# Paired 256-token blocks per PSUM bank, HGRN products on other engines, reordered small steps and placed tiles in a two-block model kernel

## The chip, the cores and the metric

One core of one Trainium2 chip. The metric is the device time of one execution in microseconds; a version is judged by the median of several executions. The profile is one further execution, taken by the hardware profiler. Its engines are TensorE (PE; its weight loads, PEld, overlap the matmuls), VectorE (DVE), ScalarE (ACT), GpSimd (POOL) and SyncE (SP, which issues the weight DMAs).

## The reference

`x` is [256 tokens, 1024]. All arithmetic is float32. The first block is a mixer and a swiglu; the second is HGRN2, swiglu, RG-LRU, swiglu; a norm stands ahead of each and at the ends of both blocks.

```python
h = rmsnorm(x, norm_mix)
proj = h @ w_in        # mamba2, block attention, forgetting attention, sliding window, gates
branches = [mamba2(...), moba(...), forgetting(...), sliding_window(...)]
x = x + sum_i(sigmoid(gate_i) * (branches[i] @ w_branch[i])) @ w_out
x = x + swiglu(rmsnorm(x), ...); x = rmsnorm(x, norm_final)
# HGRN2, 8 heads of 128:
q, fl, v, g = split(h @ hgrn_w_in); q = silu(q)
f = lb + (1 - lb) * sigmoid(fl); k = (1 - lb) * sigmoid(-fl)
S_t = diag(f_t) S_{t-1} + k_t v_t^T;  o_t = S_t^T q_t
x = x + (rmsnorm_per_head(o) * silu(g)) @ hgrn_w_out;  x = x + swiglu(rmsnorm(x), ...)
# RG-LRU:
y, u = split(h @ lru_w_in); uc = conv4(u)
r, i = sigmoid(blockdiag(uc, wa) + ba), sigmoid(blockdiag(uc, wx) + bx)
a = exp(-8 r softplus(-lam)); h_t = a h_{t-1} + sqrt(1 - a^2) i uc
x = x + (h_t * gelu(y)) @ lru_w_out; x = x + swiglu(rmsnorm(x), ...); out = rmsnorm(x, norm_final)
```

## The kernel before

The activations `x` stay on chip as two tiles of 128 tokens. Ahead of each stage `norm_input` (L199) transposes a quarter of x on TensorE, multiplies by the norm's weight on VectorE (`tsc`) and takes the sum of squares on ScalarE (L205). The norm's factor is not applied to h; it is applied where a product is evicted: as a column per token (`rstd`, L232, with the power on GpSimd, L246) or, where the tokens lie along the free axis, as a row over all partitions (`rrow`, made by L258 with two diagonal matrices `dg` and two small matmuls, L264).

Every large product is made at high precision of three matmuls per 128 rows of k: both operands are split into a rounded part and a rest (hh and hl for the activations, whi and wlo for the weights), and L154, L155, L156 are the three products (`mm3`). ScalarE casts whi and hh (L100), VectorE subtracts to wlo and hl (L101); `burst` sends the next four subtractions to GpSimd.

Weights come in units of 1 MB: a DMA on SyncE's queue into one of 4 raw buffers (`wunit`, L141), then two split tiles of 1024 columns each out of 4 (`weights`, L107). Products have two shapes. In `gemm_a` (L158) a 128 x 128 piece of h is stationary and 512 weight columns move; it serves the swiglus, the values, the gates and the output projections (where ah and al, oh and ol, loh and lol take the place of hh and hl). In `gemm_b` (L185) a 128 x 128 piece of weights is stationary and the 256 tokens of h move; each block of 128 output columns (`block_b`, L190) is 24 matmuls into the left half of a PSUM bank of its own, and is evicted by one VectorE product with `rrow`. There are 4 such banks (`acc`) and 4 more for transposes and small products (`tp`). `gemm_b` makes mamba's convolution inputs, the q and k of two attentions, HGRN's q and forget inputs (L779, L786), and RG-LRU's convolution and output gates (L930, L978).

The order of the work is set by a scheduler that runs when the kernel is built: it lists the instructions of each engine by priority (the order in which the code issues them), lets ready work of an idle engine go earlier, and is steered by `high_priority(offset)` (the splits of weights use 400, 150 in RG-LRU) and by `issue_after`, which forbids an instruction to stand ahead of another.

Around the change: `hgrn` (L748) evicts each block to one of three `u` buffers, takes a sigmoid on ScalarE (L781) and the product q on GpSimd (L782); for the forget block two sigmoids on ScalarE (L788, L789), then the affine steps on VectorE (L790, L791). `hgrn_scores` (L825) multiplies q and k on GpSimd (L834), rounds on ScalarE (L835), subtracts on GpSimd (L836), and runs levels of gated halves on VectorE (`G`, L876). `lru_rates` (L570) takes Exp and Ln of the decay parameters (L586); it is issued within the first swiglu, without a bound on how early it may go. `skew_bias` (L389) writes the bias table of 16 heads to DRAM (`relv`) and spreads it over 128 partitions into `skew` by two DMAs on GpSimd's queue, one for each attention that has such a bias (the first and the third); the attentions read their diagonals from it. `rows4` (L437) loads four heads' decay rows by a DMA on the same queue into one buffer. `conv` and `gate` in `lru` (L909) alternate four convolutions with the block-diagonal gates (L951) and the gate activations.

On-chip memory is given out pool by pool, in order: constants, x, hh and hl (`hp`), `small`, `tmp` (7168 bytes of a partition), `wraw` (32,768), `wspl`, and then the pools of a stage, such as `ffn` or `hgrn`. The weights' split tiles begin at a multiple of the tile size after `wraw`, so the distance from hh to them is the sum of the sizes between: hh and hl, `small`, `tmp` and `wraw`, 59,200 bytes.

```python
    def block_b(self, hk, wk, cs):
        n, m = len(hk), cs.stop - cs.start
        ps = self.acc()[:m, :S]
        with self.held():
            for k in range(n):
                self.mm3(ps, wk[k][0][:, cs], wk[k][1][:, cs], hk[k][0], hk[k][1], k == 0, k == n - 1)
        return ps
```

Of the kernel before, what the change touches and what calls it, by code (L numbers as in the profile page):

```python
# [20 lines left out]
EPS = 1e-6  # L21
NEG = -1.0e30
# [52 lines left out]
class Build:  # L75
    def __init__(self, tc, a):
# [8 lines left out]
        self.place = -1  # L85
        self.ahead = 400
# [111 lines left out]

    def norm_input(self, x, n, t, wcol, hi, lo, ss):  # L199
# [3 lines left out]
        junk = self.tmp.tile([P, 512], F32, tag="junk", name=self.nm("junk"), bufs=1)  # L203
        if ss is not None:
            nc.scalar.activation(junk, xc, AF.Square, accum_out=ss[:, t, n:n + 1])  # L205
# [26 lines left out]
    def rstd(self, ss, scale=1.0 / D):  # L232
# [3 lines left out]
        nc.vector.tensor_tensor(r, ss[:, :, 0], ss[:, :, 1], op=ALU.add)  # L236
        self.rsqrt(r, r, scale)
# [20 lines left out]
    def make_row(self, r):  # L258
        nc = self.nc
# [5 lines left out]
        rr = self.small.tile([P, S], F32, tag="rrow", name=self.nm("rrow"))  # L265
# [20 lines left out]
    def constants(self):  # L286
# [29 lines left out]
    def swiglu(self, hk, r, wg, g0, wu, u0, wd, x, finish, apart=0, aside=None):  # L316

        nc = self.nc
        with self.tc.tile_pool(name=self.nm("ffn"), bufs=1) as fp:
            ah = fp.tile([P, FF // P, S], F32R, name=self.nm("ah"))  # L320
            al = fp.tile([P, FF // P, S], F32R, name=self.nm("al"))
            for c0 in range(0, FF, 512):
                if c0 == 1024 and aside:
                    aside()
                n = min(512, FF - c0)
                psg, psu = self.gemm_pair(hk, wg, g0 + c0, wu, u0 + c0, n, early=c0 == 0)
                for t in range(2):
# [45 lines left out]
    def mixer(self, hk, r, rr, x, finish):  # L373
        nc, a, tc = self.nc, self.a, self.tc
        w_in = a["w_in"][0]
        with tc.tile_pool(name="yT", bufs=3) as ytp, tc.tile_pool(name="att", bufs=1) as at, \
# [12 lines left out]
            def skew_bias():  # L389
# [47 lines left out]
            def rows4(h0):  # L437
                rw = mp.tile([P, 4, S], F32, tag="rows", name=self.nm("rows"), bufs=1)
# [724 lines left out]
```

## Time and profile before

| | |
|---|---|
| Median of 3 runs | 1179.6 us (1176.96, 1179.6, 1179.66) |
| Profiled execution | 1177.61 us, span 1175.9 us |
| Mean granted clock of TensorE | 0.992 of full speed |
| TensorE busy | 1140.0 us (97% of the span), 6308 matmuls |
| VectorE busy | 737.0 us (63%) |
| ScalarE busy | 615.5 us (52%) |
| GpSimd busy | 82.1 us (7%) |
| HBM read | 200.64 MB, 174 GB/s over the span |

The span runs from the first to the last instruction of the profiled execution; its own time is 1.7 us longer. A busy TensorE is not TensorE at its peak: matmuls are pipelined, each record is longer than the distance to the next, so a pace is read from the starts. Idle time of an engine that nobody waits for costs nothing. The granted clock is the share of full speed that the chip gave TensorE in a stretch.

### The profile page before, as it was taken

To read this page: it belongs to the slowest core of one execution; us is meant where nothing else is said; L and a number is where in the kernel's file an instruction comes from. 1 tells how busy PE (TensorE), PEld (TensorE's weight loads), DVE (VectorE), ACT (ScalarE), POOL (GpSimd) and SP (SyncE) were. 2 spreads that over 40 slices of the span, in tenths; PEclk is the share of its full clock that TensorE was granted. 3 is DMA by queue.
4 is the path that set the end of the run, shared out by engine and by line. 5 is a ranking of instruction groups with operands and counts; after the bars stand their busy time and mean duration, and the time that the engine had idled before them with its cause. 6 is when DMAs were issued, how large, how long until landed. Compare 5 with 4: busy or idle time off the path is not lost.

```text
span 1175.9 us, 15771 instructions
## 1 busy us (share of the span) xinstructions
PE 1140.0 (97%) x6308; PEld 981.0 (83%) x6308; DVE 737.0 (63%) x971; ACT 615.5 (52%) x909; POOL 82.1 (7%) x87
## 2 busy tenths in 40 slices
PE   7999999999999999998999999999999879999997
PEld 7899897888888888888989878888889778888886
DVE  6976555566575555556898676555458767555552
ACT  6646647654455444446542465444446876444441
POOL 1100010000000000006520140000000000000000
PEclk9999999999999999999999999999999989999999
DMA  9785245446555555456353337554554536555440
GB/s 299 188 265 190 87 144 188 162 147 206 184 192 184 181 186 186 172 179 204 112 179 108 108 108 251 183 195 177 197 167 156 179 120 214 185 179 179 163 159 36
DMA packets 120761, 202.78 MB, mean 172 GB/s; under 512 B 4244, under 2 KB 44437, under 8 KB 120688
## 3 DMA queue, kind: packets, MB, share of 16 engines
q1 hardware_dynamic: 117264, 192.59, 50.0%
q0 software_dynamic: 2992, 8.56, 2.6%
q8 instruction: 49, 0.80, 0.3%
q10 hardware_dynamic: 432, 0.63, 0.2%
q14 instruction: 24, 0.20, 0.0%
HBM read 200.64 MB, written 4.25 MB: 174 GB/s over the span
## 4 chain that ended last, share of the span: by engine, by line
PE 84%; ACT 6%; DVE 5%; DMA 3%; issue 2%; POOLq 0%; POOL 0%; SPq 0%; ACTq 0%; DVEq 0%
PE acc L154 25%; PE acc L156 25%; PE acc L155 25%; DMA raw<-in_w_in_dram 2%; DVE wlo L101 2%; PE tp L274 2%; PE tp L865 2%; ACT whi L100 2%; PE tp L695 1%; PE tp L208 1%; DVE G L876 1%; PE tp L724 1%; PE tp L732 0%; DMA rows<-acd 0%; PE tp L731 0%
## 5 line engine op out<-in xcount | busy, mean ns | idle before, releaser
L101 DVE TENSOR_TENSOR wlo<-raw,whi 128x1024 fp32r<-128x1024 f32 (+3 forms) x364 | 444.2, 1225 | 303.5 <-ACT whi L100 296.9
L100 ACT CAST whi<-raw 128x1024 fp32r<-128x1024 f32 (+3 forms) x372 | 382.0, 1033 | 363.2 <-PE acc L156 294.3
L156 PE MATMUL acc<-whi,hl 128*128 128x512 f32 (+2 forms) x832 | 316.2, 381 | 0.0
L155 PE MATMUL acc<-wlo,hh 128*128 128x512 f32 (+2 forms) x832 | 313.7, 377 | 1.3 <-DVE wlo L101 1.3
L154 PE MATMUL acc<-whi,hh 128*128 128x512 f32 (+2 forms) x832 | 311.3, 378 | 1.3 <-ACT whi L100 1.1
L155 PEld LDWEIGHTS acc<-wlo,hh 128*128 128x128 f32 x832 | 156.4, 188 | 31.0 <-DVE wlo L101 2.4
L154 PEld LDWEIGHTS acc<-whi,hh 128*128 128x128 f32 x832 | 156.3, 188 | 28.7 <-ACT whi L100 1.9
L156 PEld LDWEIGHTS acc<-whi,hl 128*128 128x128 f32 x832 | 156.4, 188 | 28.1 <-issue 0.7
L154 PE MATMUL acc<-hh,whi 128*128 128x256 f32 (+1 forms) x496 | 142.2, 289 | 9.5 <-ACT rg L951 4.5
L156 PE MATMUL acc<-hh,wlo 128*128 128x256 f32 (+1 forms) x496 | 141.6, 287 | 1.9 <-DVE wlo L101 1.9
L155 PE MATMUL acc<-hl,whi 128*128 128x256 f32 (+1 forms) x496 | 141.8, 287 | 0.3 <-DVE hl L101 0.3
L154 PEld LDWEIGHTS acc<-hh,whi 128*128 128x128 f32 (+1 forms) x496 | 95.7, 194 | 12.7 <-ACT rg L951 4.7
L155 PE MATMUL acc<-wlo,ah 128*128 128x512 f32 x264 | 103.1, 391 | 0.0
L156 PE MATMUL acc<-whi,al 128*128 128x512 f32 x264 | 102.6, 389 | 0.0
L154 PE MATMUL acc<-whi,ah 128*128 128x512 f32 x264 | 102.5, 390 | 0.0
L156 PEld LDWEIGHTS acc<-hh,wlo 128*128 128x128 f32 (+1 forms) x496 | 95.6, 193 | 2.8 <-DVE wlo L101 2.6
L155 PEld LDWEIGHTS acc<-hl,whi 128*128 128x128 f32 (+1 forms) x496 | 95.8, 193 | 1.3 <-DVE hl L101 0.6
L156 PEld LDWEIGHTS acc<-whi,al 128*128 128x128 f32 x264 | 49.6, 188 | 10.2
L154 PEld LDWEIGHTS acc<-whi,ah 128*128 128x128 f32 x264 | 49.6, 188 | 10.1
L155 PEld LDWEIGHTS acc<-wlo,ah 128*128 128x128 f32 x264 | 49.6, 188 | 10.1
L100 ACT CAST ah<-tp 128x512 fp32r<-128x512 f32 (+1 forms) x36 | 19.8, 550 | 33.9 <-PE tp L274 33.9
L330 ACT ACTIVATE sg<-acc,rstd 128x512 f32<-128x512 f32 (+1 forms) x36 | 23.3, 648 | 20.4 <-PE acc L156 20.4
(306 smaller groups left out, 1250.8 us busy)
## 6 DMA issues: line engine op xcount, KB each, us to landing
raw<-in_ffn_w_in_dram SPq DMA_DIRECT2D x44, 1024.0 KB, 5.2
raw<-in_w_in_dram SPq DMA_DIRECT2D x33, 1024.0 KB, 5.1
raw<-in_ffn_w_out_dram SPq DMA_DIRECT2D x20, 1024.0 KB, 5.1
raw<-in_hgrn_w_in_dram SPq DMA_DIRECT2D x16, 1024.0 KB, 5.5
raw<-in_w_ffn_gate_dram SPq DMA_DIRECT2D x11, 1024.0 KB, 5.1
raw<-in_w_ffn_up_dram SPq DMA_DIRECT2D x11, 1024.0 KB, 5.2
raw<-in_w_ffn_down_dram SPq DMA_DIRECT2D x10, 1024.0 KB, 5.1
raw<-in_w_branch_dram SPq DMA_DIRECT2D x8, 1024.0 KB, 5.1
```

Of the source, the lines that this page charges most:

```text
L100: self.nc.scalar.copy(hi, src)
L101: (eng or self.nc.vector).tensor_tensor(lo, src, hi.bitcast(F32), op=ALU.subtract)
L154: mm(ps, sh, mh, start=start, stop=False)
L155: mm(ps, sh, ml, start=False, stop=False)
L156: mm(ps, sl, mh, start=False, stop=stop)
L208: last = nc.tensor.transpose(ps[:, j * P:(j + 1) * P], xc[:, j * P:(j + 1) * P], self.ident)
L274: nc.tensor.transpose(ps[:, j * P:(j + 1) * P], src[:, j * P:(j + 1) * P], self.ident)
L330: nc.scalar.activation(sg[:, :n], psg[t][:, :n], AF.Silu, scale=r[:, t:t + 1])
L695: nc.tensor.matmul(ps[par][:, jj * W:(jj + 1) * W], qT[pr, 2 * gi + jj, qt * P:(qt + 1) * P], kT(2 * gi + jj)[pr, :W], start=True, stop=True)
L724: nc.tensor.transpose(ps[:, i * P:(i + 1) * P], sp[:, i, b * P:(b + 1) * P], self.ident)
L865: nc.tensor.matmul(ps[:, c:c + 64], k[:, h, ts], q[:, h, ts].rearrange("p (n u l) -> p n u l", u=2, l=L)[:, :, 1], start=True, stop=True)
L876: nc.vector.tensor_tensor(G2, G[:, :, 0], G[:, :, 1], op=ALU.mult)
```

## The change

`gemm_b` makes its two blocks in one bank, block by block within each k, and all evictions of it are one VectorE product over both (`times_row`). `new_h` takes tiles 128 elements longer and puts h at element 96 (STILL, for the three swiglus) or 16 (MOVING, for the mixer, HGRN and RG-LRU). The opening's squares come behind its four transposes; the factor chains `rstd` and `row` run at priority offset 600. `lru_rates` and HGRN's lower bounds (`hgrn_floors`, now in the constant pool) stand behind the second chunk's silu of the first swiglu. The second skew copy is issued behind the first attention; the decay rows get two buffers. In HGRN the products q, pr and the subtraction pl go from GpSimd to VectorE, the affine steps from VectorE to ScalarE, the scaling of x by the earlier norm's factor from GpSimd to ScalarE and behind the projections; oh and ol come first in the pool, the masks ahead of the projections; u has two buffers of twice the size. RG-LRU's convolution inputs are two double tiles; a spacer of 32 elements (`apart`) follows.

```diff
+STILL, MOVING = 96, 16
...
     def gemm_b(self, hk, w, c0, nblk):
         wk = self.wunit(w, 0, 8, c0, nblk * P)
-        return [self.block_b(hk, wk, slice(b * P, (b + 1) * P)) for b in range(nblk)]
+        ps = self.acc()
+        n, mm = len(hk), self.nc.tensor.matmul
+        with self.held():
+            for k, (h, l) in enumerate(hk):
+                for b in range(nblk):
+                    o, (wh, wl) = ps[:, b * S:(b + 1) * S], (u[:, b * P:(b + 1) * P] for u in wk[k])
+                    mm(o, wh, h, start=k == 0 and b == 0, stop=False, skip_group_check=True)
+                    mm(o, wh, l, start=False, stop=False, skip_group_check=True)
+                    mm(o, wl, h, start=False, stop=k == n - 1, skip_group_check=True)
+        return ps[:, :nblk * S].rearrange("p (b s) -> p b s", s=S)
+
+    def times_row(self, out, ps, rr):
+        self.nc.vector.tensor_tensor(out, ps, rr.unsqueeze(1).to_broadcast([P, ps.shape[1], S]), op=ALU.mult)
...
-    def new_h(self):
-        hi = [self.hp.tile([P, 4, S], F32R, tag=f"hh{n}", name=self.nm("hh")) for n in range(2)]
-        lo = [self.hp.tile([P, 4, S], F32R, tag=f"hl{n}", name=self.nm("hl")) for n in range(2)]
+    def new_h(self, place):
+        def part(tag):
+            t = self.hp.tile([P, 4 * S + 128], F32R, tag=tag, name=self.nm(tag[:2]))
+            return t[:, place:place + 4 * S].rearrange("p (k s) -> p k s", s=S)
+        hi, lo = ([part(f"{u}{n}") for n in range(2)] for u in ("hh", "hl"))
...
-        nc.vector.tensor_tensor(r, ss[:, :, 0], ss[:, :, 1], op=ALU.add)
-        self.rsqrt(r, r, scale)
+        with self.tc.high_priority(offset=self.rush):
+            nc.vector.tensor_tensor(r, ss[:, :, 0], ss[:, :, 1], op=ALU.add)
+            self.rsqrt(r, r, scale)
...
-        rr = self.small.tile([P, S], F32, tag="rrow", name=self.nm("rrow"))
+        rr = self.small.tile([P, S], F32, tag="rrow", name=self.nm("rrow"), bufs=1)
...
                 if c0 == 1024 and aside:
-                    aside()
+                    with self.tc.issue_after(last.ins):
+                        aside()
...
-                for g in range(2):
-                    nc.gpsimd.dma_start(skew[g], relv[:, g].unsqueeze(1).to_broadcast([8, P, NV]))
+                copies(0)
...
-                rw = mp.tile([P, 4, S], F32, tag="rows", name=self.nm("rows"), bufs=1)
+                rw = at.tile([P, 4, 384], F32, tag="sp", name=self.nm("rows"), bufs=2)[:, :, :S]
...
+            copies(1)
             qT2, kT2, v2 = load_qkv(3080)
...
+            def made(g):
+                q, k, f = (hp.tile([P, 4, S], F32, tag=n, name=self.nm(n), bufs=2) for n in ("hq", "hk", "hf"))
+                for c in range(2):
+                    h0 = 4 * g + 2 * c
+                    hs = slice(2 * c, 2 * c + 2)
+                    u = hp.tile([P, 2, S], F32, tag="u", name=self.nm("u"), bufs=2)
+                    self.times_row(u, self.gemm_b(hk, w, h0 * P, 2), rr())
+                    sg = hp.tile([P, 2, S], F32, tag="sgq", name=self.nm("sgq"), bufs=1)
+                    nc.scalar.activation(sg, u, AF.Sigmoid)
+                    nc.vector.tensor_tensor(q[:, hs], u, sg, op=ALU.mult)
+                    u = hp.tile([P, 2, S], F32, tag="u", name=self.nm("u"), bufs=2)
+                    self.times_row(u, self.gemm_b(hk, w, D + h0 * P, 2), rr())
+                    nc.scalar.activation(f[:, hs], u, AF.Sigmoid)
+                    nc.scalar.activation(k[:, hs], u, AF.Sigmoid, scale=-1.0)
+                    for i in range(2):
+                        h, fj, kj = h0 + i, f[:, 2 * c + i], k[:, 2 * c + i]
+                        nc.scalar.activation(fj, fj, AF.Identity, scale=om[:, h:h + 1], bias=lb[:, h:h + 1])
+                        nc.scalar.activation(kj, kj, AF.Copy, scale=om[:, h:h + 1])
+                return q, k, f
+            qkf = [made(g) for g in range(2)]
+            for t in range(2):
+                nc.scalar.activation(x[:, t], x[:, t], AF.Copy, scale=rf[:, t:t + 1])
...
-        nc.gpsimd.tensor_tensor(pr, q.rearrange("p h t -> p (h t)"), k.rearrange("p h t -> p (h t)"), op=ALU.mult)
-        nc.scalar.copy(ph, pr)
-        nc.gpsimd.tensor_tensor(pl, pr, ph.bitcast(F32), op=ALU.subtract)
+        nc.vector.tensor_tensor(pr, q.rearrange("p h t -> p (h t)"), k.rearrange("p h t -> p (h t)"), op=ALU.mult)
+        self.split(ph, pl, pr)
...
-            xins = self.conv_inputs(lp, 4)
+            xins = self.conv_inputs(lp, 2)
+            lp.tile([P, 32], F32, name="apart")
...
-            begin(col["norm_mix"])
+            begin(col["norm_mix"], MOVING)
             for n in range(2):
                 for t in range(2):
-                    finish(n, t)
+                    self.norm_input(x, n, t, state["w"], state["hi"], state["lo"], None)
+            for n in range(2):
+                for t in range(2):
+                    self.square(x[:, t, n * 512:(n + 1) * 512], state["ss"][:, t, n:n + 1])
```

## Rows read from the trace of the kernel before

**Rows 1.** The page: busy us, share of the span, instructions.
```profile
PE 1140.0 (97%) x6308; PEld 981.0 (83%) x6308; DVE 737.0 (63%) x971; ACT 615.5 (52%) x909; POOL 82.1 (7%) x87
```

**Rows 2.** TensorE's waits: what waited, releaser, us in total, times, longest us.
```profile
PE acc L154 <- ACT rg L951: 5.3, 2, 4.5
...
PE acc L154 <- ACT uh L100: 4.0, 1, 4.0
...
PE acc L154 <- DVE u L779: 2.7, 1, 2.7
```

**Rows 3.** Stretches: us, busy PE, PEld, DVE, ACT, POOL, granted clock, DMA share, GB/s.
```profile
8.40:10.40 2.00, 0.01 (x1) 0.01 (x1) 1.62 (x7) 2.00 (x7) 0.00 (x0) 1.00 1.09 354
70.80:72.10 1.30, 0.04 (x2) 0.03 (x1) 0.69 (x3) 1.29 (x4) 0.00 (x0) 1.00 1.03 395
...
554.60:558.00 3.40, 3.40 (x19) 3.40 (x20) 2.42 (x7) 2.06 (x6) 3.40 (x4) 0.62 0.73 217
570.00:613.00 43.00, 40.16 (x263) 35.46 (x261) 41.77 (x57) 20.86 (x31) 15.06 (x8) 1.00 0.46 148
909.40:970.00 60.60, 49.38 (x339) 46.34 (x338) 42.53 (x60) 49.09 (x75) 0.00 (x0) 0.92 0.45 145
```

**Rows 4.** Timeline of TensorE (start, us): 512-column matmuls, 34 of hh, 25 of ah.
```profile
1059.86 0.39 PE L154 MATMUL acc<-whi,hh 128*128 128x512 f32 x1
...
1067.41 0.39 PE L154 MATMUL acc<-whi,hh 128*128 128x512 f32 x1
...
1132.93 0.39 PE L154 MATMUL acc<-whi,ah 128*128 128x512 f32 x1
...
1138.37 0.39 PE L154 MATMUL acc<-whi,ah 128*128 128x512 f32 x1
```

**Rows 5.** Timeline of TensorE: 25 matmuls of gemm_b in HGRN, 25 in RG-LRU.
```profile
561.76 0.28 PE L154 MATMUL acc<-hh,whi 128*128 128x256 f32 x1
...
564.48 0.28 PE L154 MATMUL acc<-hh,whi 128*128 128x256 f32 x1
...
900.88 0.28 PE L154 MATMUL acc<-hh,whi 128*128 128x256 f32 x1
...
903.70 0.28 PE L154 MATMUL acc<-hh,whi 128*128 128x256 f32 x1
```

**Rows 6.** Timeline of ScalarE in the opening.
```profile
6.74 1.28 ACT L586 ACT_TABLE_LOAD   x1
...
9.89 0.44 ACT L100 CAST whi<-raw 128x320 fp32r<-128x320 f32 x1
```

**Rows 7.** DMA issues (KB each, median us to landing): 36 to 80 us, then the page.
```profile
raw<-in_w_in_dram SPq DMA_DIRECT2D x6, 1024.0 KB, 16.3
...
raw<-in_w_in_dram SPq DMA_DIRECT2D x33, 1024.0 KB, 5.1
```

**Rows 8.** Groups, 537 to 613 us: busy us, mean ns, idle before and its releaser.
```profile
L100 ACT CAST whi<-raw 128x1024 fp32r<-128x1024 f32 x22 | 22.9, 1047 | 11.1 <-PE acc L155 5.7 <-issue 4.3 <-PE acc L156 1.1
...
L876 DVE TENSOR_TENSOR G<-hf 128x512 f32<-128x512 f32 x2 | 4.9, 2456 | 0.0
L836 POOL TENSOR_TENSOR pl<-pr,ph 128x1024 fp32r<-128x1024 f32 x2 | 4.8, 2416 | 1.9 <-ACT ph L835 1.9
...
L790 DVE TENSOR_SCALAR hf<-hf,om,lb 128x256 f32<-128x256 f32 x8 | 3.9, 482 | 2.0 <-ACT hf L788 2.0
...
L791 DVE TENSOR_SCALAR hk<-hk,om 128x256 f32<-128x256 f32 x8 | 3.2, 403 | 0.0
L789 ACT ACTIVATE hk<-u 128x256 f32<-128x256 f32 x8 | 3.2, 402 | 0.0
...
L845 DVE TENSOR_TENSOR hq<-hq,hf 128x1024 f32<-128x1024 f32 x2 | 2.4, 1210 | 0.0
```

**Rows 9.** Timeline of VectorE: the norm's factor in RG-LRU and its first use.
```profile
889.18 0.15 DVE L236 TENSOR_TENSOR rstd<-ss 128x2 f32<-128x2 f32 x1
...
897.32 1.08 DVE L930 TENSOR_TENSOR xin<-acc,rrow 128x256 f32<-128x256 f32 x3
```

More of the change, by code (lines that the diff above doesn't have):

```diff
@@ L85, in __init__ @@
         self.place = -1
+        self.rush = 600
         self.ahead = 400
@@ L196, in block_b, with square @@
         return ps
+    def square(self, xc, out):
+        junk = self.tmp.tile([P, 512], F32, tag="junk", name=self.nm("junk"), bufs=1)
+        self.nc.scalar.activation(junk, xc, AF.Square, accum_out=out)
     def norm_input(self, x, n, t, wcol, hi, lo, ss):
@@ L258, in make_row, with row_of @@
     def make_row(self, r):
+        with self.tc.high_priority(offset=self.rush):
+            return self.row_of(r)
+    def row_of(self, r):
         nc = self.nc
@@ L512, in mixer @@
             kd = at.tile([P, S], F32, name="kd")
-            for ps in self.gemm_b(hk, w_in, 5136, 1):
-                nc.vector.tensor_tensor(kd, ps, rr(), op=ALU.mult)
+            self.times_row(kd.unsqueeze(1), self.gemm_b(hk, w_in, 5136, 1), rr())
             dv = at.tile([P, 2, P], F32, name="dv")
@@ L568, in mixer, with hgrn_floors @@
             gp.__exit__(None, None, None)
+    def hgrn_floors(self):
+        nc = self.nc
+        self.floors = lb, om = [self.const.tile([P, 8], F32, name=n) for n in ("lb", "om")]
+        lbp = self.col["hgrn_lb_2"]
+        lt = self.small.tile([P, 2, 8], F32, tag="lt", name="lt", bufs=1)
+        nc.vector.tensor_tensor(lb, lbp[:, 0:8], lbp[:, 8:16], op=ALU.max)
+        for i in range(2):
+            nc.vector.tensor_tensor(lt[:, i], lbp[:, i * 8:(i + 1) * 8], lb, op=ALU.subtract)
+        nc.scalar.activation(lt, lt, AF.Exp)
+        nc.vector.tensor_tensor(om, lt[:, 0], lt[:, 1], op=ALU.add)
+        nc.vector.reciprocal(om, om)
+        nc.vector.tensor_tensor(lb, lt[:, 0], om, op=ALU.mult)
+        nc.vector.tensor_tensor(om, lt[:, 1], om, op=ALU.mult)
     def lru_rates(self):
@@ L592, in conv_inputs @@
     def conv_inputs(self, pool, n):
-        xins = [pool.tile([P, S + 3], F32, name=self.nm("xin")) for _ in range(n)]
+        xins = [pool.tile([P, 2, S + 3], F32, name=self.nm("xin")) for _ in range(n)]
         for xin in xins:
-            self.nc.vector.memset(xin[:, 0:3], 0.0)
+            self.nc.vector.memset(xin[:, :, 0:3], 0.0)
         return xins
@@ L610, in mamba @@
         bcT = mp.tile([P, 4, S], F32, name="bcT")
-        xins = self.conv_inputs(mp, 2)
+        xins = self.conv_inputs(mp, 1)
+        cmask = mp.tile([P, 3, P], F32, name="cmask")
+        nc.gpsimd.memset(cmask, 1.0)
+        for j in (0, 2):
+            nc.gpsimd.affine_select(cmask[:, j], cmask[:, j], pattern=[[1, P]], compare_op=ALU.is_ge,
+                                    fill=0.0, base=0, channel_multiplier=-1)
         for b in (4, 6, 0, 2):
-            for j, ps in enumerate(self.gemm_b(hk, w_in, 512 + b * P, 2)):
+            xin2 = xins[0]
+            self.times_row(xin2[:, :, 3:], self.gemm_b(hk, w_in, 512 + b * P, 2), rr())
+            for j in range(2):
                 blk = b + j
-                xin = xins[j]
-                nc.vector.tensor_tensor(xin[:, 3:], ps, rr(), op=ALU.mult)
+                xin = xin2[:, j]
                 cv = mp.tile([P, S], F32, tag="cv", name=self.nm("cv"), bufs=2)
@@ L976, in out @@
             def out(n):
-                for i, ps in enumerate(self.gemm_b(hk, w, n * 256, 2)):
-                    nc.vector.tensor_tensor(yg[:, 2 * n + i], ps, rr(), op=ALU.mult)
+                self.times_row(yg[:, 2 * n:2 * n + 2], self.gemm_b(hk, w, n * 256, 2), rr())
             def gelu(n):
```

107 lines of the change are left out of this document (35 added, 72 removed).

## The prediction

> **What bounds the kernel now.** I read the busy shares first, then TensorE's waits, its stretches, and last the pace inside one stretch. TensorE is busy 97% of the span [rows 1], so a part of this change can pay in three ways only: a wait of TensorE goes, a clock drop that follows a wait goes, or the matmuls themselves come closer together. VectorE, ScalarE and GpSimd matter where they hold TensorE up.
>
> The waits are few and have places [rows 2]: 5.3 us and 4.0 us behind ScalarE in the RG-LRU mixer, 2.7 us behind a VectorE eviction (u) in HGRN. The stretches show what each costs [rows 3]. In the opening TensorE does nothing for 2.0 us while ScalarE is busy for all of them. At 70.8 us it does nothing for 1.3 us. In the 3.4 us after the wait for u, from 554.6, the granted clock is 0.62 (between the two levels, 1.2 and 2.4 GHz) and 19 matmuls pass, so a wait is paid twice. From 570 to 613 VectorE is busy 41.77 of 43 us and TensorE lacks 2.84: there VectorE sets the pace. From 909.4 to 970 TensorE is busy 49.38 of 60.6 us.
>
> The pace shows a fourth loss that no wait names. Starts of 512-column matmuls with h as the stationary operand lie (1067.41 − 1059.86)/33 = 228.8 ns apart; in the down projection, fed by ah and al, (1138.37 − 1132.93)/24 = 226.7 ns [rows 4]. Same shape, same weights' buffers, no waits. What differs is where the stationary tile lies: by the pool sizes hh starts 59,200 bytes before the weight tiles, 64 over a multiple of 256; ah an exact multiple.
>
> **The change, part by part.** The sum is made against the profiled execution's 1177.61 us (span 1175.9); the median of the runs is 1179.6, so 2 us of the answer is scatter that I do not correct for.
>
> *Places (−3.8).* With STILL, hh of the three swiglus comes 59,904 bytes before the weights, an exact multiple of 256; with MOVING the distance stays at 64 over one, so the mixers gain nothing. The swiglus' in-projections have 3 × 2 × 5 full chunks × 8 k × 2 token tiles × 3 = 1440 such matmuls: 1440 × 2.1 ns = 3.0 us. Their 256-column rests are 3 × 2 × 8 × 2 × 3 = 288 matmuls. For these narrow ones the trace has no row that differs by place alone; two HGRN and RG-LRU stretches run at 2.72/24 = 113.3 and 2.82/24 = 117.5 ns [rows 5], so between 0 and 288 × 4.2 ns = 1.2 us; I take half, 0.6. Moving oh first in its pool puts it at an exact multiple too: 96 matmuls at 2.1 ns, 0.2. The ends: nothing, and 4.4.
> The trace says that distance matters [rows 4]. The Trainium skill, "SBUF — State Buffer", section "SBUF: two separate sides", says that PE waits for nobody on the memory's engine side; by that rule places are worth nothing and the sum is 3.8 us smaller. No run here varies the place alone yet.
>
> *Opening (−1.5).* ScalarE's squares and the Ln table load for the RG-LRU rates (1.28 us) stand ahead of the first weight cast, at 9.89 us [rows 6]. The change puts the squares behind and ties the rates and the HGRN floors to the first swiglu. The idle 2.0 us [rows 3] bound the gain; below, the factor r now comes later, but it is first needed when a bank is to be evicted, and with priority 600 it precedes the bulk of the casts. Late next is the weight DMA, which runs at the full 1.09 share there; so 1.5, ends 0 and 2.0. In the swiglu the moved table load costs ScalarE 1.3 us, which is hidden beside matmuls.
>
> *Bias copies (−1.0).* In 36 to 80 us the two skew copies (8 × 128 × 383 values, 1.5 MB each) and the weights share the DMA engines: a 1 MB weight takes 16.3 us, 5.1 over the kernel [rows 7]. TensorE's 1.3 us [rows 3] follow. One copy is moved behind the first attention, where it passes that attention's bias and row loads on the GpSimd queue; the third attention, a whole attention later, needs it. The scheduler may still put it right behind the first, since GpSimd is idle. Ends 0 and −2.5 (wait and clock), I take −1.0. The rows' second buffer lets a 0.5 MB load start earlier, on the same crowded engines: 0.
>
> *HGRN (−6.0).* Two blocks per bank: a block is 24 matmuls, 2.72 us [rows 5], so four banks hold 21.7 us of TensorE's work in place of 10.9, and the wait for u at 551.8 goes: 2.7. Its clock drop goes too: 19 matmuls took 3.4 us, at 113.3 ns they take 2.15: 1.25. VectorE in 537 to 613 loses the affine steps, 8 × 0.48 + 8 × 0.40 = 7.1 us, and gains pr and pl, 4 × 1.21 = 4.8, and q, 4 × 0.61 (half the 1024-wide row) = 2.4 [rows 8]. So far even. But GpSimd's pl takes 2.42 beside it, and VectorE's 512-wide G takes 2.46 where a 1024-wide product takes 1.21 [rows 8]: with GpSimd out of the way each of two such G gives back about 1.8 us, 3.7 together, and sixteen evictions become eight. Of the 2.84 that TensorE lacks I take 2.0 (ends 0 and 2.84). ScalarE takes 16 × 0.40 = 6.4 us and two 1024-wide scalings of x at a cast's 1.05 [rows 8], 8.5 in all; in 570 to 613 it is busy 20.86 of 43 [rows 3], so they are hidden, but see the last rival. The pair's eviction waits for the second block, 2.72 us later: hidden as long as a bank is free. Ends of the whole: −7 and, by that rival, a loss.
>
> *RG-LRU (−2.5).* The factor's sum is at 889.18, the first eviction that needs it at 897.32 [rows 9], 8 us in which finished blocks keep their banks. Priority pulls this chain forward, and wide evictions save VectorE starts. But the waits of 5.3 and 4.0 us are behind ScalarE, which loses nothing here: its gate activations, scans and casts stay. Ends: +2.7 (a pair's wait that lands once on the convolution) and −9.3 (both waits); I take about a quarter.
>
> *Nothing.* Floors in the constant pool, the causal mask in the mamba pool, HGRN's masks ahead of its projections on GpSimd's queue (which the change empties), one row buffer, wide evictions in mamba and attention: TensorE has work queued beside each, and loses more only where the row buffer is rewritten before its last reader, which ends a stage earlier. The interleaved order of gemm_b changes which tile is read after which; two paces occur already [rows 5], and 57 blocks × 24 matmuls × 4.2 ns is 5.7 us between all fast and all slow, so ±5.7 at the most, taken as 0.
>
> Sum: −3.8 − 1.5 − 1.0 − 6.0 − 2.5 = −14.8, which gives 1162.8, so **1163 us**.
>
> **Rivals.**
> *Given back.* Where ScalarE or VectorE sets the pace, earlier work only waits later: opening, bias, VectorE's relief and RG-LRU give nothing; places and the bank remain, 3.8 + 2.7 + 1.25. For: ScalarE busy 2.00 of 2.00 and VectorE 41.77 of 43 in their stretches [rows 3]. Against: the removed work stands exactly there. 1170 us. Chance 0.16.
> *Places worth nothing.* The 2.1 ns come from something else that ah and hh do not share. Against: same shape, 33 and 24 matmuls at an even pace [rows 4]. 1177.6 − 11.0 = 1167 us. Chance 0.05. (This is also what the page named above would say.)
> *More than that.* Opening and bias in full, and RG-LRU's stalls nearly all, since its clock drop goes with them: 0.5 + 1.5 + 6.8 more, 1154 us. For: each wait there drags a low clock. Chance 0.09.
> *Slower.* In HGRN ScalarE works in order. The affine steps and sigmoids can stand behind weight casts that wait for TensorE to free a weight tile, TensorE's next unit waits for a bank, the bank for u, and u has two buffers now. Then each of the eight units waits a block, 2.72 us [rows 5], and HGRN's gain is gone: 1177.6 − 8.8 + 8 × 2.72 = 1190.6. It turns the sign from 6 units on (1185); with seven, **1188 us**. For: HGRN's casts already stand 5.7 us behind matmuls [rows 8]; against: ScalarE is half idle [rows 3] and two wide buffers hold as much as four narrow ones. Chance 0.10, a third of it under six units.
>
> **How the numbers follow.** The forecast has 0.60, its own range 1154 to 1171 from the ends above. A measurement of this kernel tells 0.3% (3.5 us) from no change, so faster ends at 1176.1 and slower begins at 1183.1. Forecast, places and more are faster (0.74); of "given back" 0.11 is faster and 0.05 within; of "slower" 0.07 is slower and 0.03 within: 0.85, 0.08, 0.07. The range leaves out the slower rival (0.10), half of "more" and the tails: 1150 to 1177.
>
> **What would show it.** Right: L154 starts 226.7 ns apart in the three in-projections; no wait for u; GpSimd with no wide products in HGRN, its 512-wide G near 0.7 us; a first weight cast before 9 us; the weights' landing below 16 us in 36 to 80. Wrong: TensorE waits in HGRN that end with ScalarE's sigmoid or affine step; a pace of gemm_b at 117 ns throughout; RG-LRU's two waits unchanged or longer.

## The result and the profile after

The changed kernel took 1158.33 us (median of 4 runs, 1156.59 to 1160.06), the kernel before in the same comparison 1178.88: a ratio of 0.9828, 95% interval 0.9808 to 0.9848. That is 20.5 us faster; the forecast was 1163 in 1150 to 1177. The direction and the range held, the sum was 4.7 us short, and not where a reader of the prediction would look for it.

The profiled execution took 1156.59 us, the fastest of the four, with a span of 1154.5. Six stages end with a residual addition on VectorE. Its last one in each stage, in the timeline of VectorE (start in us, duration):

```profile
343.71 0.69 DVE L380 TENSOR_TENSOR x<-acc,x 128x512 f32<-128x512 f32 x1 [0.28 <-PE acc L158]
...
531.00 0.69 DVE L380 TENSOR_TENSOR x<-acc,x 128x512 f32<-128x512 f32 x1 [0.67 <-PE acc L158]
...
681.46 0.68 DVE L380 TENSOR_TENSOR x<-acc,x 128x512 f32<-128x512 f32 x1
...
868.66 0.68 DVE L380 TENSOR_TENSOR x<-acc,x 128x512 f32<-128x512 f32 x1
...
961.84 0.69 DVE L380 TENSOR_TENSOR x<-acc,x 128x512 f32<-128x512 f32 x1
...
1147.79 0.69 DVE L380 TENSOR_TENSOR x<-acc,x 128x512 f32<-128x512 f32 x1 [1.23 <-PE acc L158]
```

In the kernel before:

```profile
350.17 0.69 DVE L355 TENSOR_TENSOR x<-acc,x 128x512 f32<-128x512 f32 x1 [0.29 <-PE acc L156]
...
538.09 0.69 DVE L355 TENSOR_TENSOR x<-acc,x 128x512 f32<-128x512 f32 x1 [0.67 <-PE acc L156]
...
698.91 0.68 DVE L355 TENSOR_TENSOR x<-acc,x 128x512 f32<-128x512 f32 x1
...
886.80 0.68 DVE L355 TENSOR_TENSOR x<-acc,x 128x512 f32<-128x512 f32 x1
...
982.27 0.69 DVE L355 TENSOR_TENSOR x<-acc,x 128x512 f32<-128x512 f32 x1
...
1169.17 0.69 DVE L355 TENSOR_TENSOR x<-acc,x 128x512 f32<-128x512 f32 x1 [1.23 <-PE acc L156]
```

The differences of neighbours give each stage its share, beside what the prediction had for it:

| Stage | before | after | change | forecast |
|---|---|---|---|---|
| mixer with the opening | 350.2 | 343.7 | −6.5 | −2.5 |
| three swiglus | 187.9, 187.9, 186.9 | 187.3, 187.2, 186.0 | −2.3 | −3.6 |
| HGRN | 160.8 | 150.5 | −10.4 | −6.2 |
| RG-LRU | 95.5 | 93.2 | −2.3 | −2.5 |

Each column is one execution, and the one after the change is the fastest of its four. In e1 to e3, e11 and e12 below, whose edits leave HGRN alone, that stage took 151.4 us. RG-LRU took 93.6 to 95.0 in e1 to e3, e6, e7 and e11, whose edits leave it alone, and 97.8 in e10, which is the kernel before with an edit in the mixer. So about 1 us of HGRN's gain hangs on the pace of this one execution (told of at the end), and RG-LRU's gain lies anywhere between 0.5 and 4.6.

The page's first part shows TensorE busy for 10 us less and GpSimd for 30% less [rows 1]:

```profile
PE 1129.9 (98%) x6308; PEld 975.1 (84%) x6308; DVE 725.5 (63%) x932; ACT 622.9 (54%) x915; POOL 57.1 (5%) x73
```

Of TensorE's waits [rows 2] the one for u is gone; the two behind ScalarE stay, one longer, one shorter:

```profile
PE acc L156 <- ACT rg L990: 5.9, 2, 5.1
...
PE acc L156 <- ACT uh L102: 2.5, 2, 2.2
```

The stretches that answer to [rows 3] (us, busy PE, PEld, DVE, ACT, POOL, granted clock, DMA share, GB/s):

```profile
8.20:10.40 2.20, 1.84 (x9) 1.06 (x8) 2.20 (x7) 2.20 (x6) 0.19 (x1) 1.00 1.09 364
70.00:80.00 10.00, 10.00 (x85) 9.78 (x84) 8.25 (x14) 4.37 (x6) 0.00 (x0) 1.00 0.98 315
...
560.00:597.00 37.00, 37.00 (x244) 33.48 (x242) 36.73 (x51) 25.68 (x36) 0.00 (x0) 1.00 0.59 191
880.00:949.00 69.00, 60.55 (x438) 57.12 (x438) 54.29 (x77) 57.09 (x86) 0.00 (x0) 0.95 0.46 146
```

In HGRN's projections and values TensorE is now busy all the time, although VectorE is as full as it was. The RG-LRU stretch still lacks 8.45 us.

HGRN's groups of instructions answer to [rows 8] (busy us, mean ns, idle before):

```profile
L835 ACT ACTIVATE hf<-hf,lb,om 128x256 f32<-128x256 f32 x8 | 4.3, 589 | 0.0
L836 ACT ACTIVATE hk<-hk,om 128x256 f32<-128x256 f32 x8 | 3.6, 496 | 0.0
...
L914 DVE TENSOR_TENSOR G<-hf 128x512 f32<-128x512 f32 x2 | 1.4, 710 | 1.1 <-ACT hf L835 1.1
```

G went from 2456 to 710 ns, as forecast. The affine steps cost 589 and 496 ns on ScalarE; the prediction had taken 402.

The pace, in the last swiglu's in-projection: 34 wide and 49 narrow matmuls, first and last of each (timeline of TensorE).

```profile
1020.58 0.39 PE L156 MATMUL acc<-whi,hh 128*128 128x512 f32 x1
...
1028.06 0.39 PE L156 MATMUL acc<-whi,hh 128*128 128x512 f32 x1
...
1080.05 0.28 PE L156 MATMUL acc<-whi,hh 128*128 128x256 f32 x1
...
1085.81 0.28 PE L156 MATMUL acc<-whi,hh 128*128 128x256 f32 x1
```

Wide: 7.48/33 = 226.7 ns, against 228.8 [rows 4]. Narrow: 5.76/48 = 120.0 ns.

ScalarE's queue in the opening, against [rows 6]:

```profile
7.71 0.63 ACT L218 ACTIVATE junk<-x 128x512 f32<-128x512 f32 x1
...
8.34 0.44 ACT L102 CAST whi<-raw 128x320 fp32r<-128x320 f32 x1
```

The first weight cast comes 1.55 us earlier. But the fourth square (`junk`) still stands ahead of it: the scheduler put the squares back where they were. It did the same with the copies (timeline of GpSimd's queue):

```profile
44.92 2.22 POOL L429 DMA_DIRECT2D skew<-relv  x2 [4.38 <-DMA relv<-rv]
```

Both skew copies go out together. Two of the change's moves were thus not made at all, and the mixer gained more than twice its forecast.

The norm's factor in RG-LRU (timeline of VectorE, against [rows 9]):

```profile
871.02 0.16 DVE L262 TENSOR_TENSOR rstd<-ss 128x2 f32<-128x2 f32 x1
...
880.50 0.69 DVE L204 TENSOR_TENSOR xin<-acc,rrow 128x512 f32<-128x512 f32 x1 [0.71 <-PE acc L199]
```

9.5 us from the sum to the first eviction, where it was 8.1: the eviction now waits for its second block. With the priority offset at 0 (e4) the same two lie as far apart, 877.18 to 886.65 us, so the priority of the factor brought nothing here.

### The profile page after: what moved, and what is told of

It is laid out like the page before. It is cut to its first block, busy times and chain, and to the rows that moved or that the text cites. A ratio compares the mean times of both kernels' runs of the same rounds, so it can differ in the third digit from the quotient of the medians.

```text
span 1154.5 us, 15679 instructions
## 1 busy us (share of the span) xinstructions
PE 1129.9 (98%) x6308; PEld 975.1 (84%) x6308; DVE 725.5 (63%) x932; ACT 622.9 (54%) x915; POOL 57.1 (5%) x73
## 3 DMA queue, kind: packets, MB, share of 16 engines
q1 hardware_dynamic: 117264, 192.59, 50.9%
## 4 chain that ended last, share of the span: by engine, by line
PE 92%; ACT 4%; DVE 2%; issue 1%; DMA 0%; SPq 0%; POOLq 0%; POOL 0%; ACTq 0%
PE acc L158 24%; PE acc L156 24%; PE acc L157 24%; PE acc L198 4%; PE acc L197 4%; PE acc L199 4%; PE tp L304 2%; PE tp L903 2%; ACT whi L102 1%; PE tp L743 1%; PE tp L228 1%; DVE wlo L103 1%; PE tp L772 1%; PE tp L780 0%; PE tp L779 0%
## 5 line engine op out<-in xcount | busy, mean ns | idle before, releaser
L103 DVE TENSOR_TENSOR wlo<-raw,whi 128x1024 fp32r<-128x1024 f32 (+3 forms) x364 | 438.1, 1210 | 299.3 <-ACT whi L102 292.6
L199 PE MATMUL acc<-hh,wlo 128*128 128x256 f32 x456 | 128.0, 281 | 0.0
L198 PE MATMUL acc<-hl,whi 128*128 128x256 f32 x456 | 127.8, 281 | 0.0
L197 PE MATMUL acc<-hh,whi 128*128 128x256 f32 x456 | 127.4, 281 | 0.0
L199 PEld LDWEIGHTS acc<-hh,wlo 128*128 128x128 f32 x456 | 86.3, 189 | 0.4 <-issue 0.3
L198 PEld LDWEIGHTS acc<-hl,whi 128*128 128x128 f32 x456 | 86.3, 189 | 0.4
L197 PEld LDWEIGHTS acc<-hh,whi 128*128 128x128 f32 x456 | 86.1, 190 | 0.6 <-issue 0.3
```

Source lines behind the costliest of these rows:

```text
L103: (eng or self.nc.vector).tensor_tensor(lo, src, hi.bitcast(F32), op=ALU.subtract)
L197: mm(o, wh, h, start=k == 0 and b == 0, stop=False, skip_group_check=True)
L198: mm(o, wh, l, start=False, stop=False, skip_group_check=True)
L199: mm(o, wl, h, start=False, stop=k == n - 1, skip_group_check=True)
```

## The experiments

All medians below are of 4 or more runs, each compared with runs of the kernel before on the same chip; the changed kernel stands at 1158.33. The kernel before had medians of 1176.9 to 1178.9 us in these groups, so a microsecond between two groups means nothing.

### Places: e1, e8 and e9

```diff
-STILL, MOVING = 96, 16
+STILL, MOVING = 16, 16
```

> The changed kernel with STILL set to 16, so that h of the swiglus lies 64 bytes over a multiple of 256 from the weights, as before the change. Theory (place decides the pace): starts of the 512-column matmuls with stationary h go from 226.7 back to 228.8 ns, 1440 x 2.1 = 3.0 us lost; the 288 narrow ones, which the changed kernel runs at 120.0 where before they ran at 117.8, give 0.6 back; in all +2.4 us on 1158.3. Rival (place is worth nothing, the swiglus gain by something else): the paces stay at 226.7 and 120.0 and the time within 0.5 us.

1160.57 us (ratio 0.9853, 0.9839 to 0.9868): 2.2 us slower. The same matmuls in its timeline:

```profile
1024.43 0.39 PE L156 MATMUL acc<-whi,hh 128*128 128x512 f32 x1
...
1031.98 0.39 PE L156 MATMUL acc<-whi,hh 128*128 128x512 f32 x1
...
1084.20 0.28 PE L156 MATMUL acc<-whi,hh 128*128 128x256 f32 x1
...
1089.85 0.28 PE L156 MATMUL acc<-whi,hh 128*128 128x256 f32 x1
```

7.55/33 = 228.8 ns and 5.65/48 = 117.7 ns. Place decides the pace, and it does so with opposite signs for these two widths. The rival that places are worth nothing falls.

The mixers' places, `MOVING`, were then set to an exact multiple (e8) and to a distance of 192 (e9).

```diff
-STILL, MOVING = 96, 16
+STILL, MOVING = 96, 96
```

> The changed kernel with MOVING set to 96 as well, so that h of the mixer, HGRN and RG-LRU lies an exact multiple of 256 bytes from the weights. Theory (place decides the pace of both shapes, and an exact multiple is good for 512 columns and bad for 256, as the swiglus' rests at 120.0 show): the 768 wide matmuls of these stages go from 228.8 to 226.7 ns, 1.6 us won; the 57 x 24 = 1368 narrow ones from 113 to 118 up to 120, 3 to 9 us lost; the time rises by 2 to 7 us. Rival (for narrow matmuls with the weights stationary an exact multiple is as good as for wide ones): 1 to 2 us faster.

1162.82 us (0.9873, 0.9858 to 0.9888), 4.5 slower. Narrow matmuls in HGRN run 120.0 ns apart, wide ones there mostly at 227 (median). The theory holds.

```diff
-STILL, MOVING = 96, 16
+STILL, MOVING = 96, 48
```

> The changed kernel with MOVING set to 48: the distance from h to the weights in the mixer, HGRN and RG-LRU is 192 over a multiple of 256 where it was 64, so seen from the weights 64 where it was 192. So far narrow matmuls ran at 120.0 for 0, at 117.8 for 64 with h stationary, and at 113 or 118 for the changed kernel's place with the weights stationary; wide ones at 226.7 for 0 and 228.8 for 64. Theory (each distance has one pace per shape, whichever operand is stationary): the narrow ones go to 118 throughout, about +3 us. Rival (what counts is the order of the two): another pace, up to 3 us faster if all run at 113.

1162.60 us (0.9875, 0.9854 to 0.9896), 4.3 slower: narrow ones at 118 (median) in HGRN, RG-LRU and the mixer, as the theory said, and the wide ones of the mixer and HGRN at 233 to 234, which it had not asked. Its profile also holds 1.6 us of the clock drop that is told of at the end. So 16 is the best of the three for the moving side, and 96 for the still side, of those tried.

### The opening: e2 and e4

```diff
                 if c0 == 1024 and aside:
-                    with self.tc.issue_after(last.ins):
-                        aside()
+                    aside()
```

> The changed kernel without the bound that ties the RG-LRU rates and the HGRN floors to the first swiglu, so that they may go early again. Theory (the opening's gain is the table load that left ScalarE's queue; the squares are still ahead of the first weight cast in the trace after): the first weight cast goes back from 8.3 us by about 1.5, TensorE's first product with it, and the time rises by 2.5 to 3.5 us. Rival (the gain is the factor's priority and the squares' new place): under 0.5 us.

1164.67 us (0.9887, 0.9872 to 0.9902): 6.3 us slower, twice the theory. ScalarE's timeline shows where both halves come from:

```profile
6.46 1.28 ACT L626 ACT_TABLE_LOAD   x1
...
9.61 0.44 ACT L102 CAST whi<-raw 128x320 fp32r<-128x320 f32 x1
...
74.02 1.05 ACT L102 CAST whi<-raw 128x1024 fp32r<-128x1024 f32 x1 [4.11 <-DMA raw<-in_w_in_dram]
74.97 0.52 ACT L698 ACTIVATE mt<-mt 128x384 f32<-128x384 f32 x1
```

The table load pushes the first cast to 9.61, which is 1.27 us. The rest is lost at 70 to 80 us: the skew copies go out at 50.9 in place of 44.9 us, the weights that share the DMA engines with them come later, ScalarE's cast waits 4.11 us for them at 74.02, and mamba's mask exponential (`mt`), which needs no weights, is queued behind it. TensorE waits 1.8 us for that mask, and its clock falls: over the stretch from 70 to 80 us it is 0.93, with TensorE busy 8.19 us, against 1.00 and 10.00 above.

```diff
-        self.rush = 600
+        self.rush = 0
```

> The changed kernel with priority offset 0 in place of 600 for the norm factors. Theory (the factor chains are hidden; RG-LRU's gain of 2.8 us comes from paired evictions): within 1 us of 1158.3. Rival (the earlier factor is what RG-LRU, HGRN and the opening gained by): +2 to +4 us, in the first 30 us of the stages that start with a row factor.

1163.41 us (0.9877, 0.9861 to 0.9894), 5.1 slower. "Within 1 us" was wrong, and so is the rival's place: RG-LRU's stage is no slower than in the other experiments. Its first product starts at 8.72 us, no later than the changed kernel's. Beside the changed kernel's profile it has lost 3 us by 180 us, by the same course as e2 (copies at 50.4 us, a wait for the mask of 1.1 us), and 1.6 at 180 to 190 in a clock drop that is told of at the end; the rest lies within the scatter of the stages.

### The stall at 70 us: e3, e10 and e11

```diff
-                rw = at.tile([P, 4, 384], F32, tag="sp", name=self.nm("rows"), bufs=2)[:, :, :S]
+                rw = mp.tile([P, 4, S], F32, tag="rows", name=self.nm("rows"), bufs=1)
```

> The changed kernel with one buffer for the decay rows, as before. Theory (TensorE's wait at 70.8 us before the change stood behind the second load of the rows, which waited for the one buffer, not behind crowded weight loads): the second load goes back to some 60 to 67 us, TensorE waits 1 to 2 us for a small VectorE product of those rows and its clock falls after; +3.5 to +4.5 us. Rival (the gain at 70 to 80 us comes from weights or paired banks): under 1 us.

1168.84 us (0.9924, 0.9909 to 0.9938), 10.5 us slower: more than any other part of the change (in the profiles, 8.0 us by 180 us and 1.6 in the clock drop told of at the end). VectorE's timeline, GpSimd's queue and TensorE's waits:

```profile
75.86 0.35 DVE L697 TENSOR_SCALAR mt<-rows,tcol 128x256 f32<-128x256 f32 x1 [9.35 <-DMA rows<-acd]
```

```profile
64.86 0.81 POOL L476 DMA_DIRECT2D bias<-skew  x1 [18.07 <-DMA skew<-relv]
65.67 0.57 POOL L466 DMA_DIRECT2D rows<-acd  x1
```

```profile
PE tp L702 <- DVE mt L700: 5.7, 1, 5.7
```

The second load of the rows goes out at 65.7 us, lands at 75.7 among the bias and weight loads, and TensorE waits 5.7 us for the masks made of it. Its buffer had been read for the last time at 61.0 us; since then the load stood on GpSimd's queue behind the first bias load, which waited for the skew copies. With two buffers both loads of rows go out from 33.3 us on, ahead of the copies. So the price of the one buffer holds some of the copies' too, and no run parts the two. From 70 to 80 us TensorE is busy 4.27 of 10 us at a granted clock of 0.82.

Does that mean the wait before the change was the rows' too? The same buffer was given to the kernel before, alone:

```diff
-                rw = mp.tile([P, 4, S], F32, tag="rows", name=self.nm("rows"), bufs=1)
+                rw = at.tile([P, 4, 384], F32, tag="sp", name=self.nm("rows"), bufs=2)[:, :, :S]
```

> The kernel before the change with two buffers for the decay rows (of the shape and place that the change gives them) and nothing else. Theory (the wait at 70.8 us before and the low clock behind it stand behind the second load of the rows): 3 to 4.5 us faster, to about 1174.5. Rival (ScalarE's weight casts, in order ahead of the mask's exponentials, wait there for weights that come 20 us after their issue, whatever the rows do, and only the changed kernel's earlier start takes that away): within 1 us of before.

1179.24 us against 1176.91, a ratio of 1.0017 (1.0002 to 1.0033): no gain. The theory falls, and the rival's size is what was measured. ScalarE's timeline in this kernel:

```profile
70.34 1.05 ACT L100 CAST whi<-raw 128x1024 fp32r<-128x1024 f32 x1 [3.43 <-DMA raw<-in_w_in_dram]
...
72.71 0.94 ACT L651 ACTIVATE mt<-mt 128x384 f32<-128x384 f32 x2
```

and in the changed one:

```profile
63.47 0.94 ACT L699 ACTIVATE mt<-mt 128x384 f32<-128x384 f32 x2
...
68.81 1.06 ACT L102 CAST whi<-raw 128x1024 fp32r<-128x1024 f32 x1 [0.70 <-DMA raw<-in_w_in_dram]
```

Before, the exponential of the masks stands behind a cast that waits for late weights; after, it stands ahead of it. There are two gates in a row: the cast that blocks ScalarE's queue, and the rows. Opening only the second gives nothing (e10). With the first open, the second is worth 10.5 us (e3). Which part of the change opens the first is not shown: in e2 to e4 the exponentials start at 63.2 to 65.3 us as well, each time ahead of the cast that waits for weights.

Last, the second skew copy was really held back, behind the first attention's second bias load:

```diff
-            copies(1)
+            with tc.issue_after(self.drawn.ins):
+                copies(1)
```

(`self.drawn` is that load.)

> The changed kernel with the second skew copy bound behind the first attention's second bias load, so that it really goes late (in the changed kernel it still goes out at 46.1 us, 1.1 us behind the first). Theory (the first copy alone crowds the engines for half as long, but the changed kernel has no wait of TensorE left there): the weights issued at 49 to 60 us land 5 us or more earlier, the time moves by less than 1 us. Rival (the second copy is only moved into a crowd at 100 to 120 us, or the third attention waits for it): 1 to 5 us slower. A third way (the clock drops that are left there go): 1 to 2 us faster.

1158.44 us (0.9841, 0.9821 to 0.9861), no change that can be told from noise, as the theory said: the copy goes out at 99.8 us, the 1 MB weights of 36 to 80 us land in 7.3 us in place of 14.3 (medians), and the time stays. TensorE was busy for all of 48 to 80 us with and without it, so nothing was left to win.

### HGRN: e5, e6 and e7

```diff
+        return [self.block_b(hk, wk, slice(b * P, (b + 1) * P)) for b in range(nblk)]
...
-        self.nc.vector.tensor_tensor(out, ps, rr.unsqueeze(1).to_broadcast([P, ps.shape[1], S]), op=ALU.mult)
+        for b, ps in enumerate(blocks):
+            self.nc.vector.tensor_tensor(out[:, b], ps, rr, op=ALU.mult)
```

> The changed kernel with each 256-token block in a PSUM bank of its own and an eviction of its own, as before; all else stays, the double u buffers too. Theory (HGRN gained 9.5 us, of which the bank is worth 4: the wait for a bank and the clock drop behind it): +4 us in HGRN, some more in the first 40 us of RG-LRU and of the mixer if the pairs were what freed banks there, +4 to +7 in all. Rival (the factor comes early enough and VectorE is free enough that four banks do): under 1 us.

1165.23 us (0.9891, 0.9877 to 0.9906), 6.9 slower, at the theory's upper end. The wait for u is back, and the stretch behind it shows what it drags (TensorE's waits, then a stretch with the columns of [rows 3]):

```profile
PE acc L156 <- ACT uh L102: 4.0, 1, 4.0
PE acc L156 <- DVE u L195: 3.4, 1, 3.4
```

```profile
544.00:552.00 8.00, 4.63 (x27) 4.44 (x26) 3.37 (x6) 7.06 (x11) 5.01 (x13) 0.79 0.57 188
```

The edit also undoes the interleaved order of gemm_b; the narrow matmuls of HGRN lose nothing by that (median 113 ns). By the residual additions HGRN takes 156.9 us in place of 150.5 (and 151.4 in e12, so about 1 us of the difference is scatter). RG-LRU's 94.9 is no longer than in the runs that keep the pairs; what shows there is the wait for uh, 4.0 us again as before the change, where the changed kernel has 2.5.

```diff
-                    nc.vector.tensor_tensor(q[:, hs], u, sg, op=ALU.mult)
+                    nc.gpsimd.tensor_tensor(q[:, hs], u, sg, op=ALU.mult)
...
-        nc.vector.tensor_tensor(pr, q.rearrange("p h t -> p (h t)"), k.rearrange("p h t -> p (h t)"), op=ALU.mult)
-        self.split(ph, pl, pr)
+        nc.gpsimd.tensor_tensor(pr, q.rearrange("p h t -> p (h t)"), k.rearrange("p h t -> p (h t)"), op=ALU.mult)
+        self.split(ph, pl, pr, nc.gpsimd)
```

> The changed kernel with HGRN's products q and pr and the subtraction pl back on GpSimd; the affine steps and the scaling of x stay on ScalarE. Theory (GpSimd's wide operations hold up VectorE, which sets the pace there): VectorE's 512-wide G goes back from 0.71 to about 2.4 us, TensorE waits again between the projections and the values; +2 to +5 us, all of it in HGRN. Rival (VectorE is freed of as much as it is held up; the gain is the bank's): under 0.5 us.

1163.66 us (0.9876, 0.9860 to 0.9893), 5.3 slower. A group in HGRN, then GpSimd's and VectorE's timelines, and a stretch:

```profile
L914 DVE TENSOR_TENSOR G<-hf 128x512 f32<-128x512 f32 x2 | 3.4, 1705 | 1.1 <-ACT hf L835 1.1
```

```profile
569.65 3.24 POOL L103 TENSOR_TENSOR pl<-pr,ph 128x1024 fp32r<-128x1024 f32 x1 [0.20 <-ACT ph L102]
```

```profile
570.56 2.37 DVE L914 TENSOR_TENSOR G<-G 128x16 f32<-128x16 f32 x1
```

```profile
560.00:600.00 40.00, 36.88 (x243) 33.12 (x242) 38.02 (x41) 25.37 (x38) 14.02 (x6) 1.00 0.43 137
```

One of the two G is slow again (2.72 us), the mean is 1.7, and TensorE lacks 3.1 of 40 us. The delay is not a matter of size: a gate step of 16 columns beside GpSimd's `pl` takes 2.37 us, where the changed kernel's takes 0.17 with GpSimd idle. The evictions of u from PSUM take 680 ns on average beside GpSimd and 679 alone in this run. So GpSimd holds up products of two SBUF tiles here, and not the evictions.

```diff
-                        nc.scalar.activation(fj, fj, AF.Identity, scale=om[:, h:h + 1], bias=lb[:, h:h + 1])
-                        nc.scalar.activation(kj, kj, AF.Copy, scale=om[:, h:h + 1])
+                        nc.vector.tensor_scalar(fj, fj, om[:, h:h + 1], lb[:, h:h + 1], op0=ALU.mult, op1=ALU.add)
+                        nc.vector.tensor_scalar(kj, kj, om[:, h:h + 1], None, op0=ALU.mult)
...
-                nc.scalar.activation(x[:, t], x[:, t], AF.Copy, scale=rf[:, t:t + 1])
+                nc.gpsimd.tensor_scalar(x[:, t], x[:, t], rf[:, t:t + 1], None, op0=ALU.mult)
```

(and the diff of e6)

> As the run before it, and the affine steps back on VectorE and the scaling of x back on GpSimd: all four of HGRN's engine moves undone, with paired banks kept. Theory (the moves together are worth HGRN's 9.5 us less the bank's 4): +5.5 us, of which the run before has most. Rival (moving the affine steps to ScalarE costs what it saves): the same as the run before within 0.5 us.

1164.53 us (0.9886, 0.9872 to 0.9902), 6.2 slower and 0.9 behind e6. The runs of the two overlap (1162.55 to 1165.48 and 1164.15 to 1164.72), so whether the affine steps and the scaling of x gain anything stays open; the products account for nearly all of it.

### A better order: e12

The longest wait left is TensorE's 5.1 us for rg. From 909 us ScalarE loads the table of the square root, takes two, loads the table of gelu, takes two, casts, loads the table of the sigmoid, and only then empties a first bank of gates. The next product of RG-LRU is one that VectorE empties.

```diff
+            out(2)
             gate(2, uk[2], done)
-            out(2)
             last = gate(3, uk[3], done)
```

> The changed kernel with RG-LRU's third output product (out(2), 48 matmuls, evicted by VectorE) issued ahead of the third unit of gates (gate(2)). Theory (TensorE's 5.1 us at 911.6 stand behind ScalarE, which has two activation tables to load and four activations to do before it empties the first bank of gates; a product that VectorE empties fits into that time, 48 x 0.113 = 5.4 us): the wait for rg goes to under 1 us, the low clock behind it too, 4 to 6 us faster than the changed kernel, about 1153.5. Rival (ScalarE is what sets RG-LRU's end, busy nearly all of 900 to 917 us): TensorE waits as long a few us later, within 1 us of 1158.3; or ScalarE's casts for that product come later and it is 1 to 2 us slower.

1155.91 us, median of 5 (1154.69 to 1156.40), 0.9809 (0.9794 to 0.9823): 2.4 us faster than the changed kernel, all five runs below its four, half of what the theory gave, and the fastest of all. Its stretches (columns of [rows 3]):

```profile
911.00:917.00 6.00, 6.00 (x55) 6.00 (x54) 5.66 (x10) 5.96 (x9) 0.00 (x0) 1.00 0.84 289
917.00:930.00 13.00, 6.99 (x37) 6.34 (x36) 10.34 (x16) 8.47 (x14) 0.00 (x0) 0.65 0.40 122
```

and the changed kernel's:

```profile
911.00:917.00 6.00, 0.87 (x9) 0.68 (x7) 5.76 (x9) 5.94 (x9) 0.00 (x0) 0.97 0.64 200
917.00:930.00 13.00, 10.79 (x67) 10.43 (x68) 9.34 (x15) 7.07 (x12) 0.00 (x0) 0.76 0.35 102
```

The hole at 911 is filled, with 55 matmuls in place of 9. Then three weight casts, two convolution steps and a rounding stand ahead of the sigmoid's table, which is loaded at 919.9 in place of 915.1, and part of the hole comes back behind it (3.1 us for rg, 2.9 for uh) with the low clock. Both the theory and its rival had half of it.

## Why the prediction was right, and where not

**Places, forecast −3.8, of which −3.6 in the swiglus; measured there −2.3 (2.2 by e1).** The mechanism and the wide term were right: 228.8 to 226.7 ns on 1440 matmuls is 3.0 us. The step that failed is "I take half, 0.6" for the 288 narrow ones. Its range, 0 to 1.2 won, shut out a loss, and the loss came: 117.7 to 120.0 ns, 0.6 us. The order inside gemm_b, "taken as 0", stays open: the narrow medians of the mixer, HGRN and RG-LRU went from 117, 113 and 114 ns to 114, 113 and 114 in the changed kernel's profile, but HGRN's is 118 in e1 to e3, e11 and e12.

**Opening, forecast −1.5.** The first product starts at 8.83 us in place of 10.39, so the first microseconds give what was said. The reason is half of the one given: the table load left, the squares did not. What the step missed is that an early delay is worth more at 70 us: with the table load back the first product is 1.3 us later and the whole 6.3 (e2). The factor's priority, which was given no price of its own here, costs 5.1 when undone, 3 of it on the same way (e4).

**Bias copies, forecast −1.0.** The view was read rightly as far as it goes: before the change, ScalarE's cast and TensorE behind it wait for weights that the copies hold up. The edit credited with it does nothing (both copies at 45 us; e11). The wait went because the masks' exponentials came ahead of the blocked cast. The step that failed is that the rows' second buffer was put at 0: without it 10.5 us come back (e3). It does nothing alone (e10), which is why no row of before could show its worth: its wait was hidden behind another. By the stages, the start and the stretch of 70 to 80 us lie within the mixer's 6.5; how much each has of it no run parts.

**HGRN, forecast −6.2 with oh, measured −10.4 (−9.4 at the pace of e1 to e3).** The bank was sized at 4.0; undone it costs 6.9, of which some 5.5 in HGRN. For VectorE "I take 2.0 (ends 0 and 2.84)" failed: the products alone are worth 5.3 (e6). The upper end was TensorE's idle time in one stretch of 43 us, as if VectorE's delay stopped at its border. The working of that step (3.7 us of G won, the rest even) was nearer than the cap put on it. The slower rival, eight units waiting on ScalarE, did not come: TensorE is busy for all of 560 to 597 us.

**RG-LRU, forecast −2.5, measured −2.3.** That the sizes agree is luck: the stage's gain is known to 0.5 to 4.6 only. And the reason was wrong: "Priority pulls this chain forward" is not what happened (9.5 us from sum to first eviction, with and without it). What the pairs took is 1.5 us of the wait for uh (e5). The sign named as wrong, "RG-LRU's two waits unchanged or longer", came for one of the two: rg went from 5.3 to 5.9.

The parts do not add. Undone one by one they cost 2.2 + 6.3 + 10.5 + 5.1 + 6.9 + 6.2 = 37 us, where the change as a whole won 20.5. Three of them (e2, e3, e4) lose at the same stall at 70 us: 21.9 us between them, in a stage that gained 6.5.

So the direction and the two largest mechanisms (pairs, GpSimd out of VectorE's way) were right and sized too small, while the gain at 70 us and RG-LRU's came by other ways than those named; that the total still fell into the range owes something to luck.

The rival "given back" (1170) and the rival of places without effect (1167) are excluded by the result and by e1. "More than that" (1154) was nearer in the mixer, where it had −4.5, and no nearer in HGRN; RG-LRU's stalls, on which most of it was built, stayed. The Trainium skill ("SBUF — State Buffer", section "SBUF: two separate sides") has TensorE wait for nobody at the memory. e1 and e9 move nothing but addresses within it, and the starts of wide matmuls go from 226.7 to 228.8 ns apart in the swiglus (e1) and, by the medians, from 229 or 230 to 233 or 234 in the mixer and HGRN (e9), so here the measurement decides. The page speaks of engines that wait for one another, and not of places: what falls is what the prediction drew from it.

## What to carry to other kernels

Before a load or a buffer is priced at nothing, ask what waits behind the wait that hides it: an in-order queue with a blocked cast at its head hides the next gate completely. Read from the trace, not from the diff, whether a scheduler has really moved what the code moves. Where a bank is emptied by an engine with table loads ahead of it, give TensorE meanwhile a product that another engine empties.

## What was not expected of the hardware

The pace depends on the distance of the two operands in the partition modulo 256 bytes, for each width differently. With h stationary (weights minus h): wide ones took 226.7 ns at 0, 228.8 at 64 and 233 to 234 at 192 (medians in e9); narrow ones 120.0 at 0 and 117.7 at 64. With the weights stationary (h minus weights), narrow ones took 120.0 at 0, 118 at 64, and at 192 either 113.3 or 117.8 from one profile to another: HGRN's projections ran 274 matmuls at 113.3 in the changed kernel's profile and the same 274 at 117.8 in e1's, whose edit does not touch them, 1.2 us apart. What sets the pace there is open.

The same wait of 1.1 us for a weight cast at about 180 us is followed by a full clock in some profiles and by a lower one in others. Changed kernel, then e4, the same 14 us of work from just before that wait (columns of [rows 3]):

```profile
176.00:190.00 14.00, 12.38 (x76) 10.47 (x74) 7.18 (x9) 9.57 (x16) 0.00 (x0) 1.00 0.66 224
```

```profile
179.00:193.00 14.00, 12.38 (x69) 10.37 (x68) 7.24 (x9) 9.50 (x15) 0.00 (x0) 0.88 0.69 225
```

It costs 1.6 us and was there in e3, e4, e6, e7 and e9, not in e1, e2, e5, e8, e11 and e12. Each of these profiles is of another kernel. Within one kernel only times and mean clocks of the other executions are there: e6's four had 0.993, 0.995, 0.995 and 0.996 and took 1165.48, 1163.93, 1163.39 and 1162.55 us. That fits executions of one schedule that differ by some 3 us for these two causes together, but does not show it for the pace. A part that is worth less than that needs several runs.
